# Two buffers for the token rows of the norm statistics, in a hybrid S5 / pooling / windowed-attention encoder layer

## The chip, the cores and the metric

One Trainium2 chip, one of its cores. The metric is the time on the device in microseconds (us); the kernel before took 1631.17 us, the median of three runs (1629.35 to 1631.57). All data is fp32. A core has TensorE (PE, matmuls), VectorE (DVE), ScalarE (ACT), GpSimd (POOL) and SyncE (SP), which here only issues transfers. Each engine works through its own queue in order; ScalarE's queue holds a few transfers too, and those are the ones that this case is about.

## What is computed

One encoder layer over x of 4096 tokens by 1024 features. Only the first lines matter for the change:

```
def rms_norm(x, g):
    xf = x.astype(F32)
    y = xf * lax.rsqrt(jnp.mean(xf * xf, axis=-1, keepdims=True) + RMS_EPS)
    return (y * g.astype(F32)).astype(x.dtype)

h = rms_norm(x, pre_g)
proj = h @ w_in
su, sg, pu, pg, q, k, v, ag = jnp.split(proj, IN_SPLITS, axis=-1)
y_ssm = ssm_branch(su, ...) * jax.nn.silu(sg)
y_pool = pool_branch(pu, ...) * jax.nn.silu(pg)
y_attn = window_attention(q, k, v, sink) * jax.nn.silu(ag)
y = jnp.concatenate([y_ssm, y_pool, y_attn], axis=-1) @ w_out
return x + rms_norm(y, post_g)
```

The first norm needs, for each token, one over the root of the mean square of its 1024 features. The change is in how those mean squares are formed.

## The kernel before

**Tiling and passes.** The tokens are cut into 8 blocks of 512. The projection runs in three passes over the blocks (phase 1: pooling and SSM channels; phase 2: q, k, v with the attention; phase 3: the gates with the SSM), and the output projection follows. Each fp32 matmul is three: both operands are split into a rounded high part and a low part, and high x high, high x low and low x high are added up. In a block of phase 1, PE computes six chunks of 128 channels; each chunk is 8 k-tiles times 3 matmuls of 128x128 by 128x512 (`mm_k`, L350 to L352; the first chunk of a block in another order, L361, all high parts before the low ones).

**The order.** It is written out by hand on a clock of slots (class `Slots`, L84). A slot is six matmuls of PE, so a block is 24 slots, and block b of phase 1 begins at slot 24b. `e.at(slot, fn)` puts a step into the slot's list (L93), or into the current one where the slot is past: `max(slot, self.now)`. `e.step()` runs after each six matmuls and emits the steps of that slot into the queues of their engines. So slots set the order in each queue, and semaphores set the time. A transfer also waits until the transfer that used its completion semaphore last has landed; there are eight such semaphores (DMAHW0 to DMAHW7), taken in turn by the transfers of SP and ACT together.

**The normalised operand of block b (b from 1).** Four transposed pieces of x (`xt`, 128x2x512, `x_dma`) are loaded by SP; VectorE multiplies each by the gain and the row `RB[b]` of reciprocal roots (`x_norm`, L259, at slots 24b - 14, - 12, - 10 and - 8); ScalarE rounds the high part into `xk` (`x_split`, L270 through the helper `copy`, L173, at 24b - 13, - 11, - 4 and - 3); a slot later VectorE and GpSimd form the low part (L278, L279, through the helper `tt`, L162). Six slots after that, SP stores the split piece to DRAM (`xd`, 1 MB, L280), from where the later passes load it. There are six `xk` buffers, and a block uses four.

**The mean squares of block b (b from 2).** `p1_block(s)` calls `sched_stats(s + 2)` at slot 24s, so the statistics of block b are made during block b - 2 (L307 to L336): ScalarE issues the load of 128 token rows by 1024 features (`xs`, 512 KB, L318), squares them in place with a sum along the row (L322), and issues the next load; four such steps make the four columns of `ss`. Then VectorE forms the mean (L170 by the helper `ts`), GpSimd the power -0.5 (`rstd`), SP stores the 512 values to DRAM (`rb_store`, L339) and loads them back, spread over 128 partitions (`rb_load`, L344: the tile `rb`). Blocks 0 and 1 take their statistics another way. There is one `xs` buffer: load j + 1 can go out only when square j has read the buffer.

**What else ScalarE does in a block of phase 1:** it moves the chunks out of PSUM (`en` for the pool channels, L173; `pg`, silu, L733; `su`, L173), splits `xk`, and serves the SSM's preparation (`ssm_prep`), which runs beside blocks 0 to 7 in four rounds: VectorE forms tables (`obr`, `obi` with `otmp`, L162 and L490), PE transposes them (`pst`, L637) and multiplies them (`kp`, L659 and L661), ScalarE copies the transposes to `stg`, issues their store to DRAM (`swd<-stg`, L643), and copies `kp` to `k`, which reuses the buffer of `stg` and so waits for that store to land.

Of the kernel before, what the change touches and what calls it, by code (L numbers as in the profile page):

```python
# [10 lines left out]
F32 = mybir.dt.float32  # L11
F32R = mybir.dt.float32r
AF = mybir.ActivationFunctionType
ALU = mybir.AluOpType
PSUM = bass.MemoryType.PSUM

P = 128
SEQ = 4096
DM = 1024
# [9 lines left out]
EPS = 1.0e-6  # L29
# [4 lines left out]
C_NHALF, C_E1, C_HPI, C_ONE, C_NQ = 606, 614, 742, 743, 744  # L34
# [95 lines left out]
def hybrid_kernel(ctx, tc, A, out):  # L130
    nc = tc.nc
    V, S, PL, T = nc.vector, nc.scalar, nc.gpsimd, nc.tensor
    dma = nc.sync.dma_start
    e = Slots()
# [21 lines left out]
    cst = const.tile([P, NCST], F32, name="cst")  # L156
    gpre = const.tile([P, NK], F32, name="gpre")
    rstd = const.tile([P, NT], F32, name="rstd")
    ident = cst[:, C_ID:C_ID + P]

    def tt(eng, out, in0, in1, op):
        return eng.tensor_tensor(out=out, in0=in0, in1=in1, op=op)  # L162
# [4 lines left out]
    def ts(out, in0, s1, op0, s2=None, op1=None):  # L167
        if s2 is None:
            return V.tensor_scalar(out=out, in0=in0, scalar1=s1, scalar2=None, op0=op0)
        return V.tensor_scalar(out=out, in0=in0, scalar1=s1, scalar2=s2, op0=op0, op1=op1)  # L170
# [135 lines left out]

    def sched_stats(b):  # L307

        d0 = 24 * b - 48
        ss = []  # L310

        def load(j):
            if j == 0:
                ss.append(SQP[0].tile([P, 4], F32, tag="ms", name="ss", bufs=2))
            t = SQP[0].tile([P, DM], F32, tag="xs", name="xs", bufs=1)
            r0 = (4 * b + j) * P

            S.dma_start(out=t, in_=A["x"][r0:r0 + P, :])  # L318
            e.at(d0 + 4 * j + 4, square, j, t)

        def square(j, t):
            S.activation(out=t, in_=t, func=AF.Square, accum_out=ss[0][:, j:j + 1])  # L322
            if j < 3:
                load(j + 1)

        def mean():
            ts(ss[0], ss[0], 1.0 / DM, ALU.mult, EPS, ALU.add)

        def root():
            tt(PL, rstd[:, 4 * b:4 * b + 4], ss[0], cst[:, C_NHALF:C_NHALF + 4], ALU.pow)  # L330

        e.at(d0, load, 0, label="p1")
        e.at(d0 + 18, mean, label="p1")
        e.at(d0 + 19, root, label="p1")
        e.at(d0 + 22, rb_store, b, label="p1")
        e.at(d0 + 28, rb_load, b, label="main")  # L336

    def rb_store(s):
        dma(out=rbd[s].rearrange("(j p) -> p j", p=P), in_=rstd[:, 4 * s:4 * s + 4])  # L339
# [38 lines left out]
    SQP = [ph1.enter_context(tc.tile_pool(name="sqp", bufs=1))]  # L378
# [324 lines left out]
    def p1_block(s):  # L703
# [8 lines left out]
        if s + 2 < NB:  # L712
            sched_stats(s + 2)
# [779 lines left out]
```

## Time and profile before

| | |
|---|---|
| median of 3 runs | 1631.17 us |
| the profiled execution's own time | 1630.12 us |
| its span, first to last instruction | 1628.3 us |
| PE busy | 1570.8 us, 96% of the span |
| DVE / ACT / POOL busy | 1064.6 us (65%) / 731.1 us (45%) / 620.4 us (38%) |
| phase 1 on PE | about 0 to 296 us |
| xs loads | 24, of 512 KB, issued from 13.8 to 251.7 us |

The profile is one execution taken by the hardware profiler. PE is busy nearly all the time, so what counts is where PE waits. The chain that ended last gives 7% of the span to the `xs` loads, which is 0.07 x 1628.3 = 114 us of a chain that runs beside PE's own work for most of its length. In the tables below, "idle before <- X" means that the engine had nothing to run until X was done; such releasers are inferred from semaphores.

### The profile page before, as it was taken

The numbers are of one execution on the slowest core, as the hardware profiler recorded it, in microseconds if no ns is written. First come the engines' busy times: TensorE is split into PE (matmuls) and PEld (weight loads), VectorE is DVE, ScalarE is ACT, GpSimd is POOL, SyncE is SP. The second block draws the span as 40 slices with busy tenths as digits, with TensorE's granted clock in tenths as the row PEclk, the third lists the DMA queues.
The fourth block names the chain that finished last, engine by engine and source line by source line (L and its number), as shares of the span: only waits on it lengthen the run. The fifth ranks groups of instructions, "written<-read, shape, count | busy, mean of one in ns | idle before, by whom it ended". The sixth has DMA issues, their size and how long they took to land.

```text
span 1628.3 us, 20646 instructions
## 1 busy us (share of the span) xinstructions
PE 1570.8 (96%) x7284; PEld 1273.6 (78%) x7284; DVE 1064.6 (65%) x1983; ACT 731.1 (45%) x1544; POOL 620.4 (38%) x366
## 2 busy tenths in 40 slices
PE   7999899999999999999999999999979999999998
PEld 6787678788888888888888867767757878888876
DVE  6774666436677777777987467777856656555451
ACT  5423334236666666666776543333233233332221
POOL 0321212102232333333233156666732645454642
PEclk9999999999999999999999999999999999999999
DMA  6598899871312112212224365555655564555442
GB/s 232 169 302 264 252 289 306 291 283 57 117 66 71 66 66 86 103 66 91 97 98 149 115 225 194 183 171 182 222 158 167 169 197 144 177 170 193 156 155 78
DMA packets 131691, 267.56 MB, mean 164 GB/s; under 512 B 32386, under 2 KB 65922, under 8 KB 119812
## 3 DMA queue, kind: packets, MB, share of 16 engines
q1 hardware_dynamic: 126020, 251.57, 47.4%
q10 hardware_dynamic: 5568, 14.68, 2.7%
q8 instruction: 57, 0.93, 0.2%
q14 instruction: 46, 0.38, 0.1%
HBM read 173.25 MB, written 94.01 MB: 164 GB/s over the span
## 4 chain that ended last, share of the span: by engine, by line
PE 67%; DMA 15%; DVE 8%; issue 4%; POOL 3%; ACT 2%; SPq 1%; ACTq 0%; POOLq 0%; DVEq 0%
PE mm L350 9%; PE mm L351 9%; PE mm L352 9%; DMA xs<-in_x_dram 7%; PE po L848 5%; PE mm L361 5%; PE tp L858 5%; PE o L1264 5%; PE o L1262 5%; PE o L1263 5%; PE s L819 3%; PE s L818 3%; PE y L1071 1%; POOL ot L162 1%; DMA rawo<-in_w_out_dram 1%
## 5 line engine op out<-in xcount | busy, mean ns | idle before, releaser
L350 PE MATMUL mm<-xk,w 128*128 128x512 f32 x968 | 400.6, 414 | 2.1 <-ACT xk L268 1.3
L352 PE MATMUL mm<-xk,w 128*128 128x512 f32 x968 | 379.8, 392 | 1.3 <-DVE w L162 1.3
L351 PE MATMUL mm<-xk,w 128*128 128x512 f32 x968 | 380.2, 393 | 0.0
L162 POOL TENSOR_TENSOR ns<-ns,es 128x1536 f32<-128x1536 f32 (+1 forms) x64 | 172.4, 2694 | 409.8 <-ACT pp L173 187.0
L350 PEld LDWEIGHTS mm<-xk,w 128*128 128x128 f32 x968 | 182.7, 189 | 44.7 <-issue 7.5
L352 PEld LDWEIGHTS mm<-xk,w 128*128 128x128 f32 x968 | 182.3, 188 | 42.0 <-DVE w L162 2.2
L351 PEld LDWEIGHTS mm<-xk,w 128*128 128x128 f32 x968 | 182.7, 189 | 40.5 <-issue 9.1
L1262 PE MATMUL o<-wo,yk 128*128 128x512 f32 x512 | 201.2, 393 | 6.5 <-ACT gg L1122 6.0
L1264 PE MATMUL o<-wo,yk 128*128 128x512 f32 x512 | 201.0, 393 | 2.1 <-DVE yk L165 2.1
L820 DVE CUSTOM_DVE_ANT_0 ns<-s,cst,nsink 128x384 f32<-128x384 f32 (+1 forms) x256 | 145.8, 607 | 84.6 <-PE s L819 83.4
L1263 PE MATMUL o<-wo,yk 128*128 128x512 f32 x512 | 200.4, 391 | 0.0
L173 ACT ACTIVATE pp<-tp 128x512 fp32r<-128x512 f32 x188 | 112.2, 597 | 170.2 <-PE tp L858 169.3
L361 PE MATMUL mm<-xk,w 128*128 128x512 f32 x552 | 152.1, 420 | 13.2 <-ACT xk L173 6.3
L809 ACT ACTIVATE ns<-ns,nm 128x384 f32<-128x384 f32 (+1 forms) x256 | 152.3, 598 | 2.0 <-DVE nm L820 2.0
L162 DVE TENSOR_TENSOR pp<-tp,pp 128x512 fp32r<-128x512 f32 x188 | 129.2, 688 | 18.8 <-ACT pp L173 17.4
L361 PEld LDWEIGHTS mm<-xk,w 128*128 128x128 f32 x552 | 104.7, 196 | 45.2 <-ACT xk L173 10.3
L848 PE MATMUL po<-pp,vr 128*128 128x512 f32 x376 | 127.8, 421 | 0.0
L162 POOL TENSOR_TENSOR xk<-xt,xk 128x512 fp32r<-128x512 f32 x32 | 54.3, 1704 | 178.3 <-ACT xk L173 140.4
L858 PEld LDWEIGHTS tp<-cst,ns 128*128 128x128 f32 x752 | 93.0, 140 | 34.6 <-issue 10.1
L858 PE MATMUL tp<-cst,ns 128*128 128x128 f32 x752 | 112.7, 272 | 7.3 <-DVE pp L162 7.3
L1262 PEld LDWEIGHTS o<-wo,yk 128*128 128x128 f32 x512 | 97.1, 190 | 27.9 <-ACT gg L1122 6.5
L1264 PEld LDWEIGHTS o<-wo,yk 128*128 128x128 f32 x512 | 96.9, 189 | 23.1 <-DVE yk L165 2.6
(269 smaller groups left out, 2569.6 us busy)
## 6 DMA issues: line engine op xcount, KB each, us to landing
xk<-xd SPq DMA_DIRECT2D x60, 1024.0 KB
xd<-xk SPq DMA_DIRECT2D x32, 1024.0 KB
xt<-in_xT_dram SPq DMA_DIRECT2D x35, 512.0 KB
xres<-in_x_dram SPq DMA_DIRECT2D x32, 512.0 KB
out_dram<-ot SPq DMA_DIRECT2D x31, 512.0 KB
xs<-in_x_dram ACTq DMA_DIRECT2D x24, 512.0 KB
raw<-in_w_in_dram SPq DMA_DIRECT2D x32, 256.0 KB
yattn<-ysb SPq DMA_DIRECT2D x32, 256.0 KB
```

The source lines that it names most:

```text
L162: return eng.tensor_tensor(out=out, in0=in0, in1=in1, op=op)
L350: T.matmul(o, lhsT=w[:, 0, k], rhs=xh, start=(k == 0), stop=False)
L351: T.matmul(o, lhsT=w[:, 0, k], rhs=xl, start=False, stop=False)
L352: T.matmul(o, lhsT=w[:, 1, k], rhs=xh, start=False, stop=(k == NK - 1))
L361: T.matmul(o, lhsT=w[:, i, k], rhs=XK[b, k][h], start=(n == 0), stop=(n == 3 * NK - 1))
L809: S.activation(out=ns[:, hh, :nk], in_=ns[:, hh, :nk], func=AF.Exp, scale=-1.0, bias=nm[:, hh:hh + 1], accum_out=su[:, hh:hh + 1])
L820: V.tensor_tensor_reduce(out=ns[:, hh, :nk], in0=sp_[:, :nk], in1=cst[:, C_D + c0:C_D + c0 + nk], scale=-(2.0 ** -(h + 1)), scalar=R["nsin ...
L848: T.matmul(po, lhsT=VR[:, (ta + kb) % 8, kv], rhs=pp[:, i], start=(kb == 0 and i == 0), stop=(kb == nkb - 1 and i == 1))
L858: T.transpose(tp[:, hh], ns[:, hh, kb * P:(kb + 1) * P], ident)
L1262: T.matmul(o, lhsT=y[:, 0, ts_], rhs=WO[kk][:, 0, hs], start=first, stop=False)
L1263: T.matmul(o, lhsT=y[:, 0, ts_], rhs=WO[kk][:, 1, hs], start=False, stop=False)
L1264: T.matmul(o, lhsT=y[:, 1, ts_], rhs=WO[kk][:, 0, hs], start=False, stop=last)
```

## The change

There are two `xs` buffers, the first two loads of a block's statistics go out together, and load j + 2 is issued behind square j. The start `d0` becomes `max(24 * b - 54, 22 * (b - 2))` in place of `24 * b - 48`; the squares are written at d0 + 8 + 4j, the mean at d0 + 21, the root at d0 + 22, the store at d0 + 25 and the load of `rb` at d0 + 31. Since `sched_stats(b)` is called at slot 24b - 48, an earlier slot becomes that one. What the slots come to, counted from the start of the block in which the statistics are made:

| statistics of block | loads 0 and 1 | squares 0 to 3 | mean | load of rb |
|---|---|---|---|---|
| before, all | 0 and (behind square 0) 4 | 4, 8, 12, 16 | 18 | 28 |
| 2 | 0, 1 | 8, 12, 16, 20 | 21 | 31 |
| 3 | 0, 0 | 6, 10, 14, 18 | 19 | 29 |
| 4 | 0, 0 | 4, 8, 12, 16 | 17 | 27 |
| 5, 6, 7 | 0, 0 | 2, 6, 10, 14 | 15 | 25 |

```diff
--- before.py
+++ after.py
@@ -306,34 +306,36 @@
 
     def sched_stats(b):
 
-        d0 = 24 * b - 48
-        ss = []
+        d0 = max(24 * b - 54, 22 * (b - 2))
+        ss = SQP[0].tile([P, 4], F32, tag="ms", name="ss", bufs=2)
+        rows = {}
 
         def load(j):
-            if j == 0:
-                ss.append(SQP[0].tile([P, 4], F32, tag="ms", name="ss", bufs=2))
-            t = SQP[0].tile([P, DM], F32, tag="xs", name="xs", bufs=1)
+            rows[j] = SQP[0].tile([P, DM], F32, tag="xs", name="xs", bufs=2)
             r0 = (4 * b + j) * P
 
-            S.dma_start(out=t, in_=A["x"][r0:r0 + P, :])
-            e.at(d0 + 4 * j + 4, square, j, t)
-
-        def square(j, t):
-            S.activation(out=t, in_=t, func=AF.Square, accum_out=ss[0][:, j:j + 1])
-            if j < 3:
-                load(j + 1)
+            S.dma_start(out=rows[j], in_=A["x"][r0:r0 + P, :])
+
+        def square(j):
+            t = rows.pop(j)
+            S.activation(out=t, in_=t, func=AF.Square, accum_out=ss[:, j:j + 1])
+            if j < 2:
+                load(j + 2)
 
         def mean():
-            ts(ss[0], ss[0], 1.0 / DM, ALU.mult, EPS, ALU.add)
+            ts(ss, ss, 1.0 / DM, ALU.mult, EPS, ALU.add)
 
         def root():
-            tt(PL, rstd[:, 4 * b:4 * b + 4], ss[0], cst[:, C_NHALF:C_NHALF + 4], ALU.pow)
-
-        e.at(d0, load, 0, label="p1")
-        e.at(d0 + 18, mean, label="p1")
-        e.at(d0 + 19, root, label="p1")
-        e.at(d0 + 22, rb_store, b, label="p1")
-        e.at(d0 + 28, rb_load, b, label="main")
+            tt(PL, rstd[:, 4 * b:4 * b + 4], ss, cst[:, C_NHALF:C_NHALF + 4], ALU.pow)
+
+        for j in range(2):
+            e.at(d0 + j, load, j, label="p1")
+        for j in range(4):
+            e.at(d0 + 8 + 4 * j, square, j, label="p1")
+        e.at(d0 + 21, mean, label="p1")
+        e.at(d0 + 22, root, label="p1")
+        e.at(d0 + 25, rb_store, b, label="p1")
+        e.at(d0 + 31, rb_load, b, label="main")
 
     def rb_store(s):
         dma(out=rbd[s].rearrange("(j p) -> p j", p=P), in_=rstd[:, 4 * s:4 * s + 4])
```

How the queues change, at three places. ScalarE during block 2, where the statistics of block 4 are made (each `xs` row is a load, a buffer of token rows, or its square; `en` and `pg` move pool chunks out of PSUM, `xk` is the split for block 3). Before:

```order
L318 DMA xs_949<-in_x_dram 128x1024 [waits DMAHW5_49,Activation_49]
L322 ACTIVATE xs_949,ss_948<-xs_949 128x1024 [waits DMAHW5_49]
L318 DMA xs_995<-in_x_dram 128x1024 [waits DMAHW7_49,Activation_49]
L173 ACTIVATE en_1031<-mm_940 128x512 [waits PE_49]
L322 ACTIVATE xs_995,ss_948<-xs_995 128x1024 [waits DMAHW7_49]
L318 DMA xs_1061<-in_x_dram 128x1024 [waits DMAHW3_49,Activation_49]
L173 ACTIVATE en_1085<-mm_981 128x512 [waits DMAHW6_49,PE_49]
L173 ACTIVATE xk_1094<-xt_969 128x1024 [waits DMAHW1_49,DMAHW4_49,DVE_49,Pool_49]
L322 ACTIVATE xs_1061,ss_948<-xs_1061 128x1024 [waits DMAHW3_49]
```

And with the change:

```order
L317 DMA xs_949<-in_x_dram 128x1024 [waits DMAHW6_49,Activation_49]
L317 DMA xs_951<-in_x_dram 128x1024 [waits DMAHW0_49,Activation_49]
L321 ACTIVATE xs_949,ss_940<-xs_949 128x1024 [waits DMAHW6_49]
L317 DMA xs_994<-in_x_dram 128x1024 [waits DMAHW2_49,Activation_49]
L173 ACTIVATE en_1033<-mm_941 128x512 [waits DMAHW5_49,PE_49]
L321 ACTIVATE xs_951,ss_940<-xs_951 128x1024 [waits DMAHW0_49]
L317 DMA xs_1063<-in_x_dram 128x1024 [waits DMAHW5_49,Activation_49]
L173 ACTIVATE en_1087<-mm_983 128x512 [waits PE_49]
L173 ACTIVATE xk_1096<-xt_971 128x1024 [waits DMAHW1_49,DMAHW4_49,DVE_49,Pool_49]
```

The squares keep their places among the other work; each load but the first stands one square earlier, and the first split of `xk` still has two squares ahead of it.

ScalarE during block 3, where the statistics of block 5 are made, from their first load to the first split for block 4 (`k2` is the copy of the SSM's `kp`; right ahead of these rows stand the store `swd<-stg` and the copy `su1`, in both kernels). Before:

```order
L318 DMA xs_1267<-in_x_dram 128x1024 [waits DMAHW6_49]
L173 ACTIVATE k2_1291<-kp_1253 16x4x128 [waits DMAHW4_49,PE_49]
L173 ACTIVATE k2_1291<-kp_1253 16x4x112
L322 ACTIVATE xs_1267,ss_1266<-xs_1267 128x1024 [waits DMAHW6_49,Pool_49]
L318 DMA xs_1307<-in_x_dram 128x1024 [waits DMAHW1_49,Activation_49]
L173 ACTIVATE en_1325<-mm_1246 128x512 [waits DMAHW2_49,PE_49]
L322 ACTIVATE xs_1307,ss_1266<-xs_1307 128x1024 [waits DMAHW1_49]
L318 DMA xs_1347<-in_x_dram 128x1024 [waits Activation_49]
L173 ACTIVATE en_1365<-mm_1294 128x512 [waits PE_49]
L173 ACTIVATE xk_1373<-xt_1282 128x1024 [waits DMAHW2_49,DVE_49,Pool_49]
```

And with the change:

```order
L317 DMA xs_1267<-in_x_dram 128x1024 [waits DMAHW7_49]
L317 DMA xs_1269<-in_x_dram 128x1024 [waits DMAHW0_49]
L321 ACTIVATE xs_1267,ss_1246<-xs_1267 128x1024 [waits DMAHW7_49,Pool_49]
L317 DMA xs_1287<-in_x_dram 128x1024 [waits DMAHW3_49,Activation_49]
L173 ACTIVATE k2_1298<-kp_1254 16x4x128 [waits DMAHW5_49,PE_49]
L173 ACTIVATE k2_1298<-kp_1254 16x4x112
L321 ACTIVATE xs_1269,ss_1246<-xs_1269 128x1024 [waits DMAHW0_49]
L317 DMA xs_1328<-in_x_dram 128x1024 [waits Activation_49]
L173 ACTIVATE en_1330<-mm_1247 128x512 [waits DMAHW2_49,PE_49]
L321 ACTIVATE xs_1287,ss_1246<-xs_1287 128x1024 [waits DMAHW3_49]
L173 ACTIVATE en_1368<-mm_1301 128x512 [waits DMAHW4_49,PE_49]
L173 ACTIVATE xk_1376<-xt_1284 128x1024 [waits DMAHW2_49,DVE_49,Pool_49]
```

Here square 0 comes ahead of the copy `k2`, and three squares (0, 1 and 2) stand ahead of the first split, where two stood.

SP's queue in block 1, where the row `rb` of block 2 is loaded back (`xd` is the store of a split piece). Before:

```order
L344 DMA rb_676<-rbd_62 128x512 [waits DMAHW5_49,DMAHW4_49,DMAHW1_49]
L229 DMA xt_678<-in_xT_dram 128x1024 [waits DMAHW2_49,DVE_49,Pool_49]
L723 DMA pud_66<-en_621 128x512 [waits DMAHW3_49,DVE_49]
L280 DMA xd_68<-xk_587 128x2048
L280 DMA xd_68<-xk_591 128x2048 [waits DMAHW6_49]
L229 DMA xt_706<-in_xT_dram 128x1024 [waits DMAHW0_49,DVE_49,Pool_49]
L280 DMA xd_68<-xk_603 128x2048 [waits DMAHW1_49]
```

And with the change:

```order
L229 DMA xt_678<-in_xT_dram 128x1024 [waits DMAHW1_49,DVE_49,Pool_49]
L725 DMA pud_66<-en_621 128x512 [waits DMAHW3_49,DVE_49]
L280 DMA xd_68<-xk_586 128x2048 [waits DMAHW4_49]
L280 DMA xd_68<-xk_590 128x2048 [waits DMAHW6_49]
L229 DMA xt_703<-in_xT_dram 128x1024 [waits DMAHW0_49,DVE_49,Pool_49]
L280 DMA xd_68<-xk_602 128x2048 [waits DMAHW1_49]
L346 DMA rb_717<-rbd_62 128x512 [waits DMAHW2_49]
```

The load of `rb` for block 2 has moved behind three stores.

## Rows read from the trace of the kernel before

**Rows 1.** Windows of the trace: block 4 and block 6 of phase 1 on PE.

```profile
core 0: us, PE busy (x) PEld busy (x) DVE busy (x) ACT busy (x) POOL busy (x), PEclk, DMA share, GB/s
174.00:220.00 46.00, 38.83 (x169) 30.58 (x168) 30.91 (x51) 16.28 (x28) 11.86 (x6) 0.93 0.97 285
260.00:296.00 36.00, 36.00 (x171) 29.68 (x170) 22.81 (x38) 8.56 (x16) 6.73 (x5) 1.00 1.00 304
```

**Rows 2.** PE's waits from 95 to 230 us: total us, times, longest.

```profile
PE mm L361 <- DVE xk L162: 4.0, 3, 2.6
PE pst L637 <- DVE obr L162: 3.1, 1, 3.1
PE mm L361 <- ACT xk L173: 3.1, 3, 1.9
PE kp L661 <- DVE ss L170: 2.7, 1, 2.7
PE kp L659 <- DVE obr L162: 0.8, 1, 0.8
```

**Rows 3.** All engines' waits from 0 to 300 us, two lines.

```profile
ACT xs L322 <- DMA xs<-in_x_dram: 90.5, 20, 11.3
...
PE fold L424 <- ACT wt L173: 3.5, 1, 3.5
```

**Rows 4.** Timeline of ACT in block 2: start, us, instruction, idle before it.

```profile
116.63 1.06 ACT L322 ACTIVATE xs<-xs 128x1024 f32<-128x1024 f32 x1 [11.32 <-DMA xs<-in_x_dram]
...
117.81 0.33 ACTq L318 DMA_DIRECT2D xs<-in_x_dram  x1
...
124.97 1.06 ACT L322 ACTIVATE xs<-xs 128x1024 f32<-128x1024 f32 x1 [6.17 <-DMA xs<-in_x_dram]
```

**Rows 5.** Timeline of DVE in block 2.

```profile
128.16 0.69 DVE L162 TENSOR_TENSOR xk<-xt,xk 128x512 fp32r<-128x512 f32 x1 [6.18 <-ACT xk L173]
```

**Rows 6.** Windows of the trace: six us behind a stall, in blocks 3 and 5.

```profile
140.00:146.00 6.00, 6.00 (x25) 4.85 (x24) 5.97 (x7) 2.11 (x4) 3.87 (x3) 0.72 0.90 155
224.00:230.00 6.00, 5.71 (x16) 4.09 (x17) 5.97 (x8) 4.08 (x10) 2.84 (x2) 0.72 1.32 198
```

**Rows 7.** Timeline of PE: end of block 2, start of block 4.

```profile
130.61 0.66 PE L637 MATMUL pst<-cst,obi 128*128 128x128 f32 x4 [0.44 <-DVE obi L162]
...
173.98 1.07 PE L361 MATMUL mm<-xk,w 128*128 128x512 f32 x4
...
189.07 0.74 PE L361 MATMUL mm<-xk,w 128*128 128x512 f32 x2 [2.63 <-DVE xk L162]
```

**Rows 8.** Timeline of ACT in block 3.

```profile
140.43 1.08 ACT L173 ACTIVATE stg<-pst 128x512 f32<-128x512 f32 x2
...
142.05 0.43 ACTq L318 DMA_DIRECT2D xs<-in_x_dram  x1
...
158.69 1.06 ACT L322 ACTIVATE xs<-xs 128x1024 f32<-128x1024 f32 x1 [3.27 <-DMA xs<-in_x_dram]
...
159.88 0.36 ACTq L318 DMA_DIRECT2D xs<-in_x_dram  x1
...
167.76 1.06 ACT L322 ACTIVATE xs<-xs 128x1024 f32<-128x1024 f32 x1 [6.82 <-DMA xs<-in_x_dram]
...
169.81 1.05 ACT L173 ACTIVATE xk<-xt 128x1024 fp32r<-128x1024 f32 x1
```

**Rows 9.** Timeline of ACT at the end of block 4.

```profile
221.42 1.06 ACT L322 ACTIVATE xs<-xs 128x1024 f32<-128x1024 f32 x1 [6.93 <-DMA xs<-in_x_dram]
```

**Rows 10.** Timeline of SP's queue in block 1.

```profile
67.22 0.37 SPq L344 DMA_DIRECT2D rb<-rbd  x1
...
73.78 2.53 SPq L280 DMA_DIRECT2D xd<-xk  x2
```

**Rows 11.** Timeline of DVE in block 1.

```profile
76.23 1.41 DVE L165 SCALAR_TENSOR_TENSOR xt<-xt,gpre,rb 128x512 f32<-128x512 f32 x2
...
83.00 0.69 DVE L162 TENSOR_TENSOR xk<-xt,xk 128x512 fp32r<-128x512 f32 x1 [2.90 <-ACT xk L173]
...
92.35 0.69 DVE L162 TENSOR_TENSOR xk<-xt,xk 128x512 fp32r<-128x512 f32 x1 [5.12 <-ACT xk L173]
```

## The prediction

> **What bounds the kernel now.** TensorE (PE) is busy 96% of the span, so I looked first for the places where it isn't. Windows cut at the first matmul of a block show that phase 1's blocks differ though their work is the same: block 4 takes 46 us, block 6 takes 36, all of it busy, with an SSM set in each [rows 1]. PE's waits from 95 to 230 us name what is late: split operands of the next block, and VectorE's SSM tables `obr`, `obi` that PE transposes and multiplies [rows 2]. None of them names the loads of token rows. Those stand one engine further back: ScalarE waits 90.5 us in 20 waits for `xs` [rows 3]. The timelines join the two. In block 2, the first square waits 11.32 us for its load and the next load leaves at 117.81, behind it; the second square waits 6.17 us more [rows 4]. The split of `xk` stands behind that square, and so VectorE, whose next step is the low part of that split, is idle 6.18 us [rows 5]; all its SSM work behind it moves, and PE meets it late.
>
> Four losses of PE follow from this, and they are the most that the change can give back:
>
> - **A**, block 2's first chunk, about 0.95 us: the three waits for `xk` of VectorE are 4.0 us, of which 2.63 at 189.07 and some 0.5 behind it are C's [rows 2, 7].
> - **B**, the SSM products early in block 3: 2.7 + 0.8 = 3.5 us of waits [rows 2]. Then PE runs busy through 140 to 146 us at a mean granted clock of 0.72, its lower level (1.2 in place of 2.4 GHz) for part of it; 0.28 x 6 = 1.7 us [rows 6]. B is 5.2 us.
> - **C**, block 4: 46 - 36 = 10 us against block 6, waits and lower clock together [rows 1].
> - **D**, block 5's first chunk: the longest wait for `xk` of ScalarE, 1.9 us [rows 2]; the split stood behind square 3, which had waited 6.93 us [rows 9]. With the clock again at 0.72 for six us, 1.7 [rows 6], D is 3.6 us.
>
> A to D are 0.95 + 5.2 + 10 + 3.6 = 19.8 us. A second load cannot help where PE waits for nothing behind a square, and later phases have no `xs` at all, so the other 1300 us stay.
>
> **The change, part by part.** No instruction is added: 24 loads, 24 squares, 6 means, roots, stores and loads of `rb` remain, so nothing is to be paid but in order and traffic.
>
> *B.* In block 2 the order shows the squares at their old places and the loads one square ahead. Square 1's load no longer leaves at 117.81 but beside load 0, so most of its 6.17 us goes; the split, and with it VectorE's chain, comes some 5.5 us earlier (6.17 less some tenths while the pair lands). PE was 3.5 us late there, so B goes whole: 5.2. Bounds: 0, if load 1 lands no earlier than before, to 5.2.
>
> *A.* Here two things meet. ScalarE's waits in block 1 go, which had cost VectorE 2.90 and 5.12 us [rows 11]. But `rb` of block 2 is loaded three slots later and behind a third store of `xd`, which left at 73.78 or later, in place of 67.22 [rows 10]. Its time to land isn't shown; it was in place at 76.23, when the norm ran without a wait, so it took at most 9.0 us. The norm is then held up to 74.1 + 9.0 - 76.2 = 6.9 us, and the 2.90 + 5.12 = 8.0 us cover that. I take half of A, 0.5; bounds 0 and 0.95.
>
> *C.* Here the diff alone misleads. The first squares of blocks 5 to 7 stand two slots behind their loads, not eight, because the start is cut off at the current slot; and three squares stand ahead of the first split where two stood. Square 2's load leaves only behind square 0, so **two landings still stand in series** ahead of the split. Before: load out at 142.05, square at 158.69 (16.6), next load at 159.88, square at 167.76 (7.9), split at 169.81: 27.8 us [rows 8]. After: 16.6 to square 0, 1.2 for it (116.63 to 117.81 [rows 4]), 7.9 for load 2 (the copy of `kp` and square 1 run beside that), 1.2 for square 2, 0.5 for `en`: 27.4. What does change is the start. The copies of the transposes ran at 140.43 [rows 8], held by square 3 and the splits behind it, though PE had made the transposes at 130.61 [rows 7]. Without the held square they and their store run as soon as those are there, and the loads leave when PE ends block 2. That is two slots behind those transposes, a slot being at most 36 / 24 = 1.5 us [rows 1]: about 133.5, 8.5 earlier. So the split comes 8.5 + 0.4 = 8.9 us earlier. Through VectorE's work behind it, PE's wait at 189.07 [rows 7] moves with it, so at the end of C the kernel is 8.9 us ahead, of which A and B are 5.7. C gives **3.2 of its 10**. Bounds: -4.7 (a split 7.9 us later, one more landing) and 10.
>
> One page bears on the size of 16.6 with two loads under way. No row shows two loads of ScalarE together, as there was one buffer; one alone took 7.2 (117.81 to 124.97) to 7.9 us [rows 4, 8]. The Trainium skill, "DMA: Bandwidth & Descriptors", section "Queues, rings and completion order", says that on each of the 16 DMA engines the descriptors of a queue are taken up in ring order; by it the second load stands behind the first and holds it back by nothing, which is the sum here; were the two to share alike, load 0 would land up to 7.9 us later, which is the rival below.
>
> *D.* Load 3 now leaves behind square 1, two other squares and two landings ahead of its use, so the 6.93 us go. D is 3.6; bounds 0 and 3.6.
>
> *Start.* Load 1 leaves beside load 0 at 14 us, ahead of the weights that hold PE 3.5 us at `fold` [rows 3], not among them. Its 512 KB may delay or spare those; I take 0, with 2 us either way.
>
> **Sum:** 0.5 + 5.2 + 3.2 + 3.6 = 12.5 us off the profiled execution's 1630.1 (span 1628.3 and 1.8 around it): 1617.6. The median of the runs was 1.05 above that execution, so 1618.7; I say **1619**. The best ends together (0.95 + 5.2 + 10 + 3.6 + 2 = 21.8) would give 1609.
>
> **The rivals.** *Half the gain.* If the pair holds its first load back by 3 us, the split of block 4 comes 5.9 earlier, and D's slack goes into the same delay: 1630.1 - 5.9 = 1624.2, as a median 1625.
>
> *All of it.* If landings are shorter when the `xs` traffic is spread, the split of block 4 is never late: 19.8 off, median 1611. Against it: the two landings in series.
>
> *No change.* The DMA engines are the real limit: their share is 0.97 in block 4 and 1.00 in block 6 [rows 1], and a load that leaves early delays the `rb` and `xt` rows that the norms need. Then the waits change names only: 1631. The Trainium skill has such a rule (same page, "Issuing engines are not separate DMA queues": all transfers run on the same 16 engines and interleave). Against it: block 6 ran at the share of 1.00 with PE fully busy.
>
> *Slower: the pair.* In blocks 3 to 5 the first square follows right behind two loads. Let d be what the second load costs the first. Up to C's end the gain is 8.9 - d; in block 5, where PE had its splits just in time, d is lost again, and D gives nothing. The kernel takes 1630.1 - 8.9 + 2d, and is slower than before when d is over 4.5 us. With d at a whole landing, 7.9, it is 1637.0, median 1638. Against it: ScalarE's queue held the long SSM store ahead of the load already, and 16.6 us has that in it.
>
> **How the numbers follow.** My forecast (gains of 8 to 16 us) 0.55; half the gain 0.14; all of it 0.08; no change 0.12; slower 0.11. Two runs of this kernel can tell apart about 0.2%, 3.3 us. Faster by more: 0.55 + 0.14 + 0.08 = 0.77; within it 0.12; slower 0.11. The range 1611 to 1632 leaves out about 0.04 below, and above it the slower case with a part of "no change", 0.15.
>
> **What would show it.** ScalarE's waits for `xs` fall from 90.5 to some 45 us: the first square of each block's four still waits, in block 3 square 2 too, the others hardly. The waits of PE at `kp` L661 and L659 are gone, the window at a clock of 0.72 behind them too; block 4 is still the longest, about 43 us in place of 46; block 5's first chunk has no wait for ScalarE. Block 6 begins about 12 us earlier, and everything behind keeps its length. I am wrong if block 4 is as short as block 6 (landings weren't the limit), if square 0 waits longer than 16.6 us in block 3 (the pair), or if VectorE's waits for `rb` (left as they are in my sum) take the place of those for `xk`.

## The result, and the profile after

The change makes the kernel slower: 1647.99 us median of 4 runs (1644.36 to 1649.23) against 1631.37 of the kernel before, run beside it (4 runs, 1629.35 to 1637.45). The ratio is 1.0086, with a 95% interval of 1.0065 to 1.0108. The profiled execution took 1647.0 us with a span of 1645.2, 16.9 more than before. Where they arise is read from the first matmul of each block on PE (L361 before, L363 after), in us:

| block | 1 | 2 | 3 | 4 | 5 | 6 | 7 | phase 2 |
|---|---|---|---|---|---|---|---|---|
| begins, before | 60.14 | 98.35 | 133.87 | 173.98 | 220.17 | 260.33 | 296.06 | 330.25 |
| begins, after | 60.58 | 98.77 | 143.53 | 184.13 | 229.53 | 273.91 | 309.64 | 349.57 |
| later by | 0.4 | 0.4 | 9.7 | 10.2 | 9.4 | 13.6 | 13.6 | 19.3 |

Three blocks lose: block 2 (9.3 us), block 5 (4.2) and block 7 (5.7); some 2.4 us come back by the end. (Phase 1 has blocks 0 to 7, so before it lasts to 330 us; "to 296", in the table of the kernel before, is where block 7 begins.) PE's waits from 95 to 230 us, the view of [rows 2]:

```profile
PE mm L363 <- ACT xk L173: 6.1, 2, 5.6
PE mm L363 <- DVE xk L162: 2.9, 2, 2.6
PE kp L663 <- DVE ss L170: 2.7, 1, 2.7
PE pst L639 <- DVE obr L162: 2.7, 2, 1.5
PE pst L639 <- DVE obi L162: 2.6, 2, 1.4
```

The wait at `kp` is still 2.7 us, and one wait of 5.64 us for a split of ScalarE is new, at 106.38 in block 2's first chunk. Around it PE's clock falls; the windows below have the columns of [rows 1]. From 103 to 110 us the mean granted clock is 0.51, the lower level (1.2 GHz) for nearly all of it, while PE had 3.62 us of work in 7. Block 4 (184 to 230) is little changed, and block 6 (274 to 310) is as whole as before.

```profile
103.00:110.00 7.00, 3.62 (x9) 2.90 (x10) 5.76 (x19) 3.82 (x6) 3.97 (x3) 0.51 0.62 78
...
184.00:230.00 46.00, 40.18 (x173) 31.26 (x172) 25.49 (x38) 14.38 (x23) 8.24 (x6) 0.93 1.01 272
...
274.00:310.00 36.00, 36.00 (x171) 29.68 (x170) 21.59 (x37) 6.90 (x13) 4.88 (x3) 1.00 1.01 274
```

What the change aimed at did happen: ScalarE waits less for `xs`, 59.1 us in 8 waits after 90.5 in 20 [rows 3]. All engines' waits, after:

```profile
ACT xs L321 <- DMA xs<-in_x_dram: 59.1, 8, 14.2
```

VectorE waits less for the splits `xk` of ScalarE, too, but more for rows. Its waits from 55 to 340 us, before:

```profile
DVE xk L162 <- ACT xk L173: 27.4, 14, 6.2
...
DVE xt L165 <- DMA rb<-rbd: 20.7, 5, 6.3
...
DVE xt L165 <- DMA xt<-in_xT_dram: 8.2, 6, 2.4
```

and after:

```profile
DVE xt L165 <- DMA xt<-in_xT_dram: 33.3, 7, 8.4
DVE xt L165 <- DMA rb<-rbd: 24.9, 2, 13.6
...
DVE xk L162 <- ACT xk L173: 2.4, 4, 0.8
```

The `rb` waits are two instead of five, but 13.6 and 11.3 us long, and the waits for the pieces `xt` of transposed x are 25 us longer in sum. The queue of SP shows why, in two places. The first is block 1, SP's timeline after (compare [rows 10]):

```profile
70.22 1.51 SPq L280 DMA_DIRECT2D xd<-xk  x2
73.38 0.33 SPq L229 DMA_DIRECT2D xt<-in_xT_dram  x1
77.16 0.32 SPq L280 DMA_DIRECT2D xd<-xk  x1
77.52 0.47 SPq L346 DMA_DIRECT2D rb<-rbd  x1
```

and then VectorE's norms of blocks 2 and 3 (compare [rows 11]), and what follows on ScalarE and PE (the timelines of DVE, of ACT and of PE):

```profile
90.36 1.41 DVE L165 SCALAR_TENSOR_TENSOR xt<-xt,gpre,rb 128x512 f32<-128x512 f32 x2 [13.61 <-DMA rb<-rbd]
...
99.26 0.68 DVE L162 TENSOR_TENSOR xk<-xt,xk 128x512 fp32r<-128x512 f32 x1
...
133.42 1.41 DVE L165 SCALAR_TENSOR_TENSOR xt<-xt,gpre,rb 128x512 f32<-128x512 f32 x2 [11.30 <-DMA rb<-rbd]
```

```profile
91.80 1.06 ACT L173 ACTIVATE xk<-xt 128x1024 fp32r<-128x1024 f32 x1 [13.22 <-DVE xt L165]
```

```profile
106.38 5.06 PE L363 MATMUL mm<-xk,w 128*128 128x512 f32 x14 [5.64 <-ACT xk L173]
```

The `rb` of block 2 leaves at 77.52 behind three 1 MB stores and a load of `xt`, and is in place at 90.36, 12.8 us later. VectorE stands, ScalarE's splits stand behind it, and PE has no operand.

The second place is the statistics of blocks 5 to 7. SP's timeline in block 4, before:

```profile
184.62 0.37 SPq L339 DMA_DIRECT2D rbd<-rstd  x1
185.04 0.63 SPq L229 DMA_DIRECT2D xt<-in_xT_dram  x1
189.08 0.32 SPq L280 DMA_DIRECT2D xd<-xk  x1
195.01 0.32 SPq L344 DMA_DIRECT2D rb<-rbd  x1
```

and after:

```profile
187.97 0.37 SPq L341 DMA_DIRECT2D rbd<-rstd  x1
188.43 0.46 SPq L280 DMA_DIRECT2D xd<-xk  x1
200.17 0.32 SPq L346 DMA_DIRECT2D rb<-rbd  x1
200.55 0.42 SPq L229 DMA_DIRECT2D xt<-in_xT_dram  x1
```

The load of `rb` reads what the 2 KB store `rbd` wrote, and waits until that has landed, some 11 to 12 us after it was issued here. Before, the first load of `xt` stood ahead of it (slot 24b - 22 against 24b - 20) and left at once. In the change the load of `rb` of blocks 5 to 7 is at slot 24b - 23, ahead of that load of `xt`, and holds it: 12.6 us from store to `xt` load in place of 0.4. SP's `rb` loads don't wait longer for these stores, 33.0 us in 4 waits from 0 to 340 us after 30.6 in 5; what has changed is which transfers stand behind the wait.

PE meets this in blocks 5 and 7, where its waits for splits are 5.0 and 4.6 us after 2.1 and 1.0:

```profile
238.37 0.73 PE L363 MATMUL mm<-xk,w 128*128 128x512 f32 x2 [3.90 <-DVE xk L162]
...
316.20 6.33 PE L363 MATMUL mm<-xk,w 128*128 128x512 f32 x16 [4.58 <-ACT xk L173]
```

The way to the second is roundabout. VectorE waits 7.12 us for `xt`, ScalarE's split behind that, and behind the split the copy `stg`, whose store leaves at 301.58. The copy of `kp` waits for that store to land and holds the next split (timelines of DVE and ACT):

```profile
298.50 1.42 DVE L165 SCALAR_TENSOR_TENSOR xt<-xt,gpre,rb 128x512 f32<-128x512 f32 x2 [7.12 <-DMA xt<-in_xT_dram]
```

```profile
300.00 1.07 ACT L173 ACTIVATE xk<-xt 128x1024 fp32r<-128x1024 f32 x1 [6.50 <-DVE xt L165]
...
314.07 1.13 ACT L173 ACTIVATE k<-kp 16x512 f32<-16x512 f32 x2 [11.46 <-DMA swd<-stg]
```

### The profile page after: what moved, and what is told of

It reads as the page before. It is cut to its first block, busy times and chain, and to the rows that moved or that the text cites. A ratio compares the mean times of both kernels' runs of the same rounds, so it can differ in the third digit from the quotient of the medians.

```text
span 1645.2 us, 20651 instructions
## 1 busy us (share of the span) xinstructions
PE 1578.1 (96%) x7284; PEld 1279.1 (78%) x7284; DVE 1060.1 (64%) x1983; ACT 731.8 (44%) x1544; POOL 620.6 (38%) x366
## 4 chain that ended last, share of the span: by engine, by line
PE 70%; DMA 12%; DVE 9%; issue 5%; POOL 3%; ACT 1%; SPq 1%; POOLq 0%; ACTq 0%; DVEq 0%
PE mm L352 9%; PE mm L353 9%; PE mm L354 9%; PE mm L363 5%; PE o L1264 5%; PE o L1266 5%; PE o L1265 5%; PE po L850 5%; PE tp L860 5%; DMA xt<-in_xT_dram 4%; PE s L821 3%; PE s L820 3%; DMA rb<-rbd 2%; PE y L1073 1%; DVE xt L165 1%
## 5 line engine op out<-in xcount | busy, mean ns | idle before, releaser
L363 PE MATMUL mm<-xk,w 128*128 128x512 f32 x552 | 154.4, 424 | 23.7 <-ACT xk L173 12.9
L363 PEld LDWEIGHTS mm<-xk,w 128*128 128x128 f32 x552 | 106.1, 199 | 56.2 <-ACT xk L173 15.9
L162 POOL TENSOR_TENSOR xk<-xt,xk 128x512 fp32r<-128x512 f32 x32 | 51.0, 1605 | 186.1 <-ACT xk L173 123.2
```

Source lines behind the costliest of these rows:

```text
L363: T.matmul(o, lhsT=w[:, i, k], rhs=XK[b, k][h], start=(n == 0), stop=(n == 3 * NK - 1))
```

## The experiments

The theory after the two traces: the loss comes from the slots, by way of the load of `rb` on SP's queue. The first rival: it comes from the pair of `xs` loads. The runs e, f, g and h were taken as four groups, each on another chip. The kernel before ran again in each, with medians of 1631.0, 1629.8, 1636.7 and 1636.7, so runs of different groups are compared by their ratios to it; 0.1% is 1.6 us. This takes it that what slows a chip slows all these kernels alike, which no run shows. By the intervals in the table, a difference of two ratios is known to about 0.3%, 4 to 5 us, either way.

| run | ratio to before | 95% interval |
|---|---|---|
| the change | 1.0086 | 1.0065 to 1.0108 |
| e1: two buffers, slots before | 0.9926 | 0.9903 to 0.9948 |
| e2: one buffer, slots of the change | 1.0140 | 1.0114 to 1.0166 |
| e3: the change, block 2 put back | 1.0039 | 1.0022 to 1.0057 |
| e4: before, `rb` of block 2 later | 1.0032 | 1.0015 to 1.0048 |
| f2: e1, load 1 beside load 0 | 0.9913 | 0.9891 to 0.9934 |
| f3: e1, block 3 in the change's slots | 0.9955 | 0.9940 to 0.9971 |
| f5: e1, blocks 4 to 7 in the change's slots | 0.9996 | 0.9980 to 1.0013 |
| f4: e2, block 2 put back | 1.0119 | 1.0095 to 1.0142 |
| g1: the change, `rb` loads put back | 0.9970 | 0.9954 to 0.9986 |
| g2: f5, `rb` loads put back | 0.9937 | 0.9913 to 0.9961 |
| g3: e1, `rb` loads of 4 to 7 earlier | 0.9983 | 0.9965 to 1.0001 |
| h1: the change, `rb` loads by GpSimd | 0.9973 | 0.9957 to 0.9988 |
| h2: f2, `rb` loads by GpSimd | 0.9910 | 0.9889 to 0.9931 |
| h3: h2, the stores too | 0.9936 | 0.9915 to 0.9957 |

**Buffers and slots apart.** e1 keeps the two buffers and takes every slot of the kernel before:

```diff
-        d0 = max(24 * b - 54, 22 * (b - 2))
+        d0 = 24 * b - 48
-            e.at(d0 + 8 + 4 * j, square, j, label="p1")
-        e.at(d0 + 21, mean, label="p1")
-        e.at(d0 + 22, root, label="p1")
-        e.at(d0 + 25, rb_store, b, label="p1")
-        e.at(d0 + 31, rb_load, b, label="main")
+            e.at(d0 + 4 + 4 * j, square, j, label="p1")
+        e.at(d0 + 18, mean, label="p1")
+        e.at(d0 + 19, root, label="p1")
+        e.at(d0 + 22, rb_store, b, label="p1")
+        e.at(d0 + 28, rb_load, b, label="main")
```

> Two buffers and the pair of loads as in the change, but squares, mean, root, store and row load in the slots of the kernel before (squares 4 slots behind, block 2's row load at slot 28). If the time is lost by the late row of block 2 (its load three slots later, issued at 77.5 us behind a third xd store, so that VectorE waited 13.6 us at 90.4): that wait is gone, block 2's first chunk ends near 98, block 3's starts within 2 us of 133.9, and the kernel takes 1615 to 1631 us. If it is lost by the pair of loads, which lengthens the DMA queue for everything behind it: 1640 us or more, with VectorE's waits for xt rows still above 20 us.

e2 is the other half: `bufs=1`, load j + 1 behind square j, the change's slots.

> The change's slots with one buffer: load j+1 behind square j, nothing loaded in pairs. Late-row theory: VectorE again waits over 10 us for block 2's row near 90 us, PE again loses about 9 us between 98 and 143 us, and the kernel takes 1640 us or more. Pair theory: without the pair the loss is gone, 1622 to 1633 us.

e1 took 1618.55 us, e2 1654.11. So the buffers alone gain 0.74%, 12.1 us, and the slots alone cost 1.4%, 22.8 us. The slots lose without any pair of loads, and a pair gains without these slots. In e1 PE's waits from 95 to 230 us are one group, the `kp` wait is gone, and ScalarE's waits for `xs` are 38.0 us in 10 (the views as above):

```profile
PE mm L363 <- DVE xk L162: 4.9, 3, 3.8
```

```profile
ACT xs L321 <- DMA xs<-in_x_dram: 38.0, 10, 12.5
```

**Block 2 alone, from both sides.** e3 puts block 2's squares to `rb` load back in the change; e4 moves one thing in the kernel before:

```diff
-        e.at(d0 + 28, rb_load, b, label="main")
+        e.at(d0 + (31 if b == 2 else 28), rb_load, b, label="main")
```

> The change, with block 2's squares, mean, root, store and row load alone put back to the slots before (4, 8, 12, 16, 18, 19, 22, 28). Late-row theory: block 2's row lands by 77 us, the next block starts within 2 us of 133.9 instead of 143.5, and at least those 9 us come back: 1639 us or less, and 1625 or less if the later losses (4.2 us behind 229, 5.7 us behind 310) follow from it too. Pair theory: within 3 us of 1648.

> The kernel before with nothing changed but the row load of block 2, three slots later (31 for 28). Late-row theory: VectorE's norm of block 2, without a wait at 76.2 us before, waits 8 us or more, and the kernel loses 6 to 12 us: 1637 to 1643 us. Pair theory: without the pair the row lands within the 6.9 us that the prediction took as its bound and the time stays at 1631 within 3 us.

e3 took 1636.74 us: block 3 begins at 133.75, and 0.47%, 7.7 us, is back, by the ratios. The losses behind it did not go with it, so they have a cause of their own. e4 took 1636.49, half a microsecond below what was expected, 0.32% or 5.2 us over before. Its profiled execution is the slowest of its 12 (1641.86). The load leaves at 76.37 there (SP), and VectorE waits as in the change:

```profile
88.79 1.42 DVE L165 SCALAR_TENSOR_TENSOR xt<-xt,gpre,rb 128x512 f32<-128x512 f32 x2 [10.70 <-DMA rb<-rbd]
```

So the price of these three slots is shown without any pair of loads.

**The blocks behind.** f2 gives e1 the change's places for loads 0 and 1 and nothing else. My expectation calls them earlier by 2 to 6 slots; that is wrong, since a step can't stand before the call at 24b - 48, and only load 1 moves, by one slot.

> Two buffers with the squares, mean, root, store and row load in the slots of the kernel before, and only the first two loads as early as in the change (2, 4, 6, 6 and 6 slots earlier for blocks 3 to 7). If the 18 us between the two-buffer kernel (1618.6) and the change with block 2 put back (1636.7) come from the squares and the store and row load behind them, this takes 1614 to 1623 us, and the blocks' lengths are those of the two-buffer kernel (34.8, 42.1, 36.7 us for blocks 3, 4, 5) within 1.5 us. If they come from the early loads (more in front of the rows in the DMA queue, or more loads under way when ScalarE issues its next): 1632 us or more, with lengths near 39.9, 46.4 and 42.0.

It took 1617.26 us, the same as e1 within the intervals: that slot of load 1 costs nothing that can be told, and what is left of the slots is squares, means, roots, stores and `rb` loads. f3 and f5 give e1 the change's slots for block 3, and for blocks 4 to 7:

> The two-buffer kernel with block 3's statistics alone in the change's slots (loads 2 earlier, squares 2 later, mean, root, store and row load 1 later). If a later square makes the store and then the row load late (POOL's root at 138.6 instead of 132.7 us, the row load issued 5.4 us later), block 3 takes 38 to 41 us instead of 34.8 and the kernel 1621 to 1627 us. If single blocks do not matter and the loss is one of the total traffic, it stays within 3 us of 1618.6.

> The change with blocks 2 and 3 put back: only blocks 4 to 7 have its slots (from block 5 on loads 6, squares 2, store and row load 3 slots earlier). If the slots of these blocks cost by themselves, blocks 4, 5 and 7 stay 3 to 6 us longer than in the two-buffer kernel each and the time is 1628 to 1634 us. If the late row of block 3 is what spoils the later blocks, their lengths go back to 42.1, 36.7 and 36.9 us and the time to 1616 to 1623 us.

Against e1, block 3's slots cost 0.29%, 4.7 us (1622.77), those of blocks 4 to 7 0.70%, 11.4 us (1629.37); against f2, which ran beside them, 0.42% and 0.83%. Both are near the sizes expected, and there is no chain reaction from block 3: blocks 4 to 7 of f3 take 151.0 us together, those of e1 151.4. In f3 block 3 takes 40.0 us for 34.8: GpSimd's root is made at 139.53 for 132.71 in e1, and the `rb` load leaves at 153.76 for 147.46. f4 is e2 with block 2's slots of before:

> One buffer (load j+1 behind square j) with the change's slots for blocks 3 to 7 and those of before for block 2. If the slots cost by themselves, whatever the buffers, as they did with two (18 us): 1643 to 1653 us against 1631. If they cost only where loads go in pairs: 1628 to 1634 us.

1650.20 us: the slots of blocks 3 to 7 cost 19.4 us with one buffer, 18.4 with two (e3 against e1). Within the intervals they don't depend on the buffers.

**Is it the `rb` load's slot?** g2 is f5 with the `rb` load of blocks 4 to 7 at 24b - 20 again; g1 is the whole change with that in all blocks; g3 is e1 with nothing but the change's `rb` load slots for blocks 4 to 7:

```diff
-        e.at(d0 + 31, rb_load, b, label="main")
+        e.at(24 * b - 20, rb_load, b, label="main")
```

> Blocks 4 to 7 in the change's slots, blocks 2 and 3 in those before (1629.4 us), now with the row loads of blocks 4 to 7 put back to slot 24b - 20, that is behind the first load of x's transposed rows on SyncE's queue, where they stood before. Held-queue theory (the row load waits on SyncE for its store to land, and with it the loads behind it; in blocks 5 to 7 the change put it ahead of the first load of x): blocks 4, 5 and 7 go back to 42, 37 and 37 us or less and the time to 1614 to 1621 us. If the earlier squares and stores cost, whatever the row load does: 1626 to 1632 us.

> The two-buffer kernel (1618.6 us) with nothing but the row loads of blocks 4 to 7 in the change's slots (27, 25, 25, 25 for 28). Held-queue theory: with the store where it was the row load waits the longer, the loads of x behind it land later, VectorE's waits for xt rise by 10 us or more, and the time is 1626 to 1636 us. If the order of the row load on SyncE costs nothing: within 3 us of 1618.6.

> The whole change with the row loads alone put back to slot 24b - 20 in all blocks (28 for 31 in block 2, 52 for 53 in block 3, 3 slots later in blocks 5 to 7); squares, mean, root and store stay where the change has them. If the place of the row load is all of the loss: 1616 to 1622 us. If block 2's and block 3's later squares and stores cost by themselves, since a row load waits on SyncE for its store: 1624 to 1640 us, with blocks 2 and 3 still longer than 34 and 35 us and blocks 4, 5 and 7 at 42, 37 and 37.

By ratios g2 gains 0.59% on f5 (9.6 us), g3 loses 0.57% on e1 (9.3 us), and g1 gains 1.16% on the change (18.9 us). The times are 1627.75, 1634.80 and 1631.43 us beside a before of 1636.68, so g2's own time is above what was written for it; its distance from before, 10.3 us, is within. By the plain medians the three are 1.6, 16.3 and 16.6 us, so g1 and g3 stand either way, while g2's gain on f5 rests on the ratios. Within the group g3, which has the change's `rb` loads alone, is 0.46% slower than g2, which has the change's other slots without them.

The block lengths that I wrote for g1 and g2 did not come: block 4 took 48.0 and 48.5 us in these two executions. In f5 the first norm in that block waits for `xt` until 193.15; in g2 it waits 11.13 us for the `rb` load that was put back, until 197.96, with the block begun 1.4 us earlier. So in that block the old place was no gain. In g3 the mechanism is plain. SP's timeline in block 5, e1 first:

```profile
210.79 0.37 SPq L341 DMA_DIRECT2D rbd<-rstd  x1
...
211.77 0.49 SPq L229 DMA_DIRECT2D xt<-in_xT_dram  x1
...
224.05 0.32 SPq L346 DMA_DIRECT2D rb<-rbd  x1
```

then g3:

```profile
221.57 0.37 SPq L341 DMA_DIRECT2D rbd<-rstd  x1
234.42 0.33 SPq L346 DMA_DIRECT2D rb<-rbd  x1
234.80 1.17 SPq L229 DMA_DIRECT2D xt<-in_xT_dram  x1
```

VectorE's waits for `xt` from 55 to 340 us are 48.3 us in 12 in g3:

```profile
DVE xt L165 <- DMA xt<-in_xT_dram: 48.3, 12, 11.2
```

In e1 they are 15.1 in 8. The sums alone don't tell the cost, though: for `rb` VectorE waits 37.3 us in 5 in e1, a fast kernel, and 24.9 in 2 in the change. In g1 the norm of block 2 runs at 76.20 with 0.65 us of wait, against 13.61 in the change.

**Held queue or late packets?** h1 is the whole change with one engine changed; GpSimd now waits for the store, and SP is free:

```diff
-        dma(out=rb, in_=bc(rbd[s:s + 1, :], [P, TB]))
+        (PL.dma_start if 2 <= b < NB else dma)(out=rb, in_=bc(rbd[s:s + 1, :], [P, TB]))
```

> The whole change, every slot of it kept, with the row loads of blocks 2 to 7 issued by GpSimd in place of SyncE (it waits there for the store, and SyncE is not held). If the loss is SyncE being held at a row load whose store has not landed, and the loads of x standing behind it: the two kernels of this change that differ by the row load's slots differ by 19 us, and that comes back, 1622 to 1632 us. If the row's packets only meet too much traffic, whoever issues them: 1640 us or more.

1631.66 us, a ratio of 0.9973: 1.13% or 18.4 us come back, as much as by moving the slots (g1). GpSimd takes over the hold (timeline of POOL):

```profile
112.19 0.60 POOL L346 DMA_DIRECT2D rb<-rbd  x1 [8.78 <-DMA rbd<-rstd]
```

This ties the loss to the `rb` loads' place in SP's queue. It does not part three effects: the `rb` load no longer holds SP, it no longer stands behind SP's stores (issued at 74.24, block 2's `rb` was in place at 82.15, after 7.9 us in place of 12.8), and it no longer takes one of the eight completion semaphores that SP and ScalarE share.

h2 and h3 try the same on f2, the fastest kernel; h3 also has GpSimd issue the stores.

> The fastest kernel so far (two buffers, loads early, everything else in the slots before: 0.9913 of the kernel before), with the row loads of blocks 2 to 7 issued by GpSimd. Held-queue theory: SyncE still waited some 37 us in 5 waits for stores to land there; without them the loads of x land earlier, VectorE's waits for xt fall, and the time is 0.980 to 0.990 of before. If GpSimd's queue costs more than SyncE's hold (its low parts of the splits stand behind the row load): 0.993 or more.

> As the one with GpSimd's row loads, with the stores of the roots issued by GpSimd too, which makes the roots itself, so that SyncE waits neither for the roots (21 us in 5 waits in the two-buffer kernel) nor for the stores. Held-queue theory: at least as fast as with the row loads alone, 0.975 to 0.990 of before. If the waits for the roots on SyncE lie beside other work: the same as with the row loads alone, within 0.2 per cent.

Both missed: 1621.81 us (0.9910, the same as f2) and 1627.79 (0.9936, none better). In h2 VectorE's waits for `xt` fell from 19.0 us in f2 to 6.2, as expected, but those for `rb` rose from 36.0 to 44.9. With the `rb` load in its old place SP's hold, 40.6 us in 5 waits in f2, probably lay beside other work. In h3 the waits for `rb` rose to 64.1 us. f2 and h2 are the fastest here, 0.9% below the kernel before; e1 is not told apart from them.

## Why the prediction was wrong

The forecast, 1619 us within 1611 to 1632, was 29 us short, and the sign was wrong.

- **The gains were there.** With the slots of before the two buffers give 12.1 us (e1); the sum was 12.5. *B*: the `kp` wait is gone in e1, and block 3 takes 34.8 us for 40.1, 5.3 less, predicted 5.2. *C*: block 4 takes 42.1 for 46.2; the text said about 43 for 46. *D*: block 5 takes 36.7 for 40.2, 3.5 less, predicted 3.6. That the totals meet is luck in part. These are lengths of single executions; f2, as fast, has 45.3 for C and 35.7 for D; and block 1 begins 1.8 us later in e1 and block 7 takes 2.7 us longer, neither of which is in the sum.
- **C's working was right by luck.** In block 3 of the change the split came 26.8 us behind the first load, for 27.4 in the sum, but in other terms: square 0 ran 5.1 us behind its load and not 16.6, and the next load then waited 10 us for the landing of an `rb` load. The load itself left at 150.32, 6.8 us into the block, and not at 133.5, the block's start.
- **The step that failed first is A**, and in it the size of the hold. The text saw the later `rb` of block 2, bounded the hold of VectorE's norm at 6.9 us, and let 8.0 us of removed ScalarE waits cover that. VectorE waited 13.61 us, and the norm began 14.1 later than before. Two terms were short. The load left at 77.52 and not at 74.1: the third store ahead of it stood 3.4 us for the landing of an `xt` load (SP's waits from 70 to 80 us), where the text took the time of that store from the kernel before. And it was in place after 12.8 us and not 9.0: a bound that was read from a row with less ahead of it was no bound. The block lost 9.3 us where the text took 0.5 as a gain; the slots of block 2 alone are worth 7.7 us (e3).
- **A's cover was nearly as large as forecast.** VectorE's waits of 2.90 and 5.12 us are gone in the change, and at its second low part of block 2 it is only 6.9 us late (99.26 for 92.35 [rows 11]). The second buffer is not what removed them: e4, with one buffer, shows the same, 12.6 us late at the norm and 5.4 at that low part (88.79 and 97.70), 1.8 of it from the start of block 1.
- **The second step was missing.** The three slots by which the `rb` loads of blocks 5 to 7 come earlier were not costed at all; the text left VectorE's waits for `rb` "as they are in my sum". Yet the order of SP's queue would have shown that load ahead of the first `xt`, and the wait for the store's landing in front of it. With block 4, where the load is one slot earlier, that place costs 9.3 us on e1 (g3), known to some 5 us either way.
- **The rest.** The later squares, roots and stores of blocks 2 and 3 are worth 5.4 us (g1 against g2), just outside the noise; by which way, no run shows. With the `rb` loads' 18.9 that is 24.3 of the 26.1 us between e1 and the change (1.6%); the 1.8 left are g2 against e1, within the noise.
- **The rivals.** "The pair", the only slower case, is refuted by f2, where loads 0 and 1 leave together, and by g1, where the squares follow right behind them as well: both are faster than before. Its sign, a square 0 more than 16.6 us behind its load in block 3, did not come either (5.1 us). "No change" had a true part, that `rb` and `xt` rows would be late, but put it down to the DMA engines and early loads; h1 moves no `xs` load, and the rows come. The rule of the Trainium skill, "DMA: Bandwidth & Descriptors", section "Queues, rings and completion order", which the text used for the pair of `xs` loads, was wanted one step further on: descriptors of a queue are taken up in ring order, so a row behind three 1 MB stores on one queue is taken up after them. The trace agrees: by its semaphore records the third store had landed at 89.78 and `rb` at 90.33, 12.8 us after its issue; from GpSimd's queue it took 7.9.
- **The signs that were written down** were partly right: waits for `xs` fell (to 59.1, not 45), and block 5's first chunk has no wait for ScalarE. The last sentence, that the prediction is wrong if VectorE's waits for `rb` take the place of those for `xk`, came near: the waits for `xk` fell by 25.0 us, those for `rb` rose by 4.2 and those for `xt`, which it does not name, by 25.1.

## What to carry to other kernels

When a diff moves the slots of a chain, follow every DMA of the chain through its issuing queue: here a small load that waited for a store to land held every transfer behind it on that queue, and its place among the large ones was worth more than its bytes. Move a resource (a buffer) and a schedule (the slots) in separate kernels, since here one gained 0.7% and the other lost 1.4% and the sum hid both. A landing time read from one row bounds only a transfer with no more ahead of it.

## What the runs showed that I had not expected

ScalarE is coupled to SP by more than data. In block 3 of the change, the load behind square 0 leaves only at 166.72, and what ends that hold is the landing of SP's `rb` load, which no instruction of ScalarE there reads. The link is one of the eight completion semaphores that the two share: by the trace's semaphore records ScalarE waits there on the one that the `rb` load of 162.18 signals, and the `xs` load takes the same one next. ACT's timeline:

```profile
166.72 0.33 ACTq L317 DMA_DIRECT2D xs<-in_x_dram  x1
167.16 1.14 ACT L173 ACTIVATE k<-kp 16x512 f32<-16x512 f32 x2 [10.56 <-DMA rb<-rbd]
```

In e1 the same load is held 11.61 us by an `xd` store, in the same way, so it is no cost of the change, but a second buffer does not free ScalarE from it. The turn of the eight shifts with every reordering, so each run here also changes which transfer waits for which; no run holds that fixed.

And the 2 KB store `rbd` slows the transfers of all queues. The kernel writes the 512 values column by column, and in the trace's packets each is one of four bytes. It took 8.4 to 12.2 us to land, before and after, by the semaphore records. Of 318 transfers that were issued while such a store of SP was under way, by any engine and in all traces, 303 landed after it. A row `rbd<-rb` of the same size, which another step stores in one piece (L456 before), had landed after 1.1 us. In the change block 2's store is three slots later and under way from 59.66 to 71.20. SP and ScalarE issued loads from 65 to 68 us in both kernels; the windows, after and then before:

```profile
65.00:70.00 5.00, 4.72 (x14) 3.76 (x15) 4.63 (x7) 1.29 (x2) 4.69 (x3) 0.66 0.28 7
```

```profile
65.00:70.00 5.00, 5.00 (x15) 3.64 (x15) 4.63 (x7) 2.21 (x3) 5.00 (x3) 0.66 0.69 203
```

That is 7 GB/s in place of 203. When such a store is issued is therefore part of what the slots change, and a rival for the 5.4 us above. No run writes the 512 values in one piece, so what this store costs the kernel, and why it holds the others, stays open.
